# One ring of six PSUM banks for both scans, in-place token loads, and a reordered first stage in a hybrid block kernel

## The chip, the cores and the metric

The program runs on one core of one Trainium2 chip. Its engines are TensorE (PE in the profile, with PEld for its weight loads), VectorE (DVE), ScalarE (ACT), GpSimd (POOL) and SyncE (SP); SP, ACT and POOL also issue transfers between HBM and the on-chip memory. The metric is device time in microseconds (us), lower is better.

## The reference

One layer over 2048 latent tokens and 256 context tokens of width 1024. Cut to what matters:

```python
p_lat = (_layer_norm(h_x) * (1.0 + sc_l[:, None]) + sh_l[:, None]) @ w_in[l]     # sc, sh: silu(c) @ mod_w + mod_b
p_ctx = (_layer_norm(h_ctx) * (1.0 + sc_c) + sh_c) @ w_in[l]
pv, u, fh, g = _split_proj(p)                                   # pooling, RWKV-7, HGRN2, gates
u = _shift3(u, rwkv_shift)                                      # a 3-tap convolution over tokens
y = _rwkv_branch(u_ctx, u_lat, ...)                             # two directions, state from the context
o = _hgrn_branch(fh_ctx, fh_lat, ...)                           # two directions, chunkwise, state from the context
pool = _pool_branch(pv, True, pool_w, pool_scale)
mix = concat([pool, y, o]) * silu(g)
new_x = _layer_norm(ALPHA * h_x + gt * (mix @ w_out)) * ln_g + ln_b

# RWKV-7, one token:  S = S * w - (S kk) (kk * a)^T + v k^T ;  y = S r
# HGRN2, one chunk:   S = exp(g_last) * S + (k * exp(g_last - g))^T i ;  o = (q * exp(g)) S + causal scores i
```

## The kernel before

All matrix products of the projections are made in three passes of a rounded high part and a rest (`wh`, `wl` of the weights; `xh`, `xl` of the tokens), so each 128x1024 block of weights is loaded, cast on ACT and subtracted on DVE or POOL before it is used.

**First stage** (lines 220 to 514). The modulation vector is `silu(c) @ mod_w`: eight loads `mt` of 1 MB on SP's queue into a pool of three buffers, four matmuls each (L241), 16 small transposes (L252), giving `mods`. Then 9 groups of 256 tokens: `x_group` normalizes, transposes on PE (L296) and scales with `mods` into `xm`; `split_group` makes `xh` and `xl`; `conv_block` makes 24 matmuls (L330) for each of 11 blocks of RWKV inputs, `low_rank(d, p, ...)` two small matmuls on the 64 partitions of direction `d` (L347), and further functions the decays, keys and values of each chunk, stored to DRAM (`s_kr`, `s_bk`, `s_vt`). The order here is made by the compiler's scheduler. In the first group each block's weights are loaded just before its `conv_block`, into the pool of three buffers that the token tiles `xt` share.

**RWKV scan** (lines 666 to 974). 36 chunks of 64 tokens in both directions at once. `start` makes the 128x384 score tiles (matmuls L720 into two PSUM banks `pa`, masked by DVE into `at`, L722) seven chunks ahead; `gather` and `solve` invert the triangular blocks of four chunks together in 62 dependent DVE operations (L777, L780) with transfers `sd`, `m`, `so`, `nn` around them; `merge` (L829, L839) and `late` (L742) finish a chunk's factors in banks of the same pool `psa` of two; `step` is the recurrence (`py` L856 and L862, `pu` L872, L881, L897, then `tz` and `zbd` on DVE) in pools `psy` and `psu` of two banks each. PE's order is written out by hand, the other engines are ordered by the scheduler. Between the pieces, `filler` makes the remaining 22 blocks of the input projection (pooling, HGRN2 inputs, gates) in three parts of 768 tokens: it loads tokens `fxs` with two buffers, splits them into `fxh`/`fxl`, and makes 24 matmuls `fps` (L567) for each block and token range. `pace` decides how many of its pieces (six matmuls each) are run per iteration: 7.6 by `R_FIL`. A border between two parts ends the piece.

**HGRN2 scan** (lines 979 to 1181). Ten iterations `n` of 14 slots: `hlevels` for window `n` (`scores`, matmuls L1043 in `pl`; POOL and DVE at L1072), `hsteps` for window `n-1` (L1087, L1102, L1105, L1115 in `pa`, `po`, `ps`, from four pools of 2, 1, 1 and 2 banks). `H_FIL` is the filler's rate per slot; the rest of the filler runs at `n` = 8. `out_weights` loads `w_out`, scales it on POOL and splits it, also at `n` = 8.

**Output stage** (lines 1184 to 1307). `readout` normalizes and gates a group of 512 tokens, `project_out` makes one tile of 128 tokens: matmuls with `w_out`, layer statistics, scaling on ACT (L1290) and POOL (L1291, L1292), one store.

## Time and profile before

| what | us |
|---|---|
| median of 3 runs | 2161.99 (2156.2 to 2167.65) |
| the profiled execution | 2169.2 |
| its span, first to last instruction | 2167.3 |
| first matmul of the first stage's blocks | 53.07 |
| recurrence of the first chunk starts | 652.1 |
| recurrence of the last chunk starts | 1388.6 |
| output stage alone, from about | 1950 |

Times on the engines are counted from the start of the span. A line such as L829 is a line of the kernel before.

### The profile page before, as it was taken

To read this page: it belongs to the slowest core of one execution; us is meant where nothing else is said; L and a number is where in the kernel's file an instruction comes from. 1 tells how busy PE (TensorE), PEld (TensorE's weight loads), DVE (VectorE), ACT (ScalarE), POOL (GpSimd) and SP (SyncE) were. 2 spreads that over 40 slices of the span, in tenths; PEclk is the share of its full clock that TensorE was granted. 3 is DMA by queue.
4 is the path that set the end of the run, shared out by engine and by line. 5 is a ranking of instruction groups with operands and counts; after the bars stand their busy time and mean duration, and the time that the engine had idled before them with its cause. 6 is when DMAs were issued, how large, how long until landed. Compare 5 with 4: busy or idle time off the path is not lost.

```text
span 2167.3 us, 46917 instructions
## 1 busy us (share of the span) xinstructions
PE 1866.9 (86%) x18498; PEld 1581.6 (73%) x18498; DVE 1439.7 (66%) x3037; ACT 930.9 (43%) x1763; POOL 797.8 (37%) x729
## 2 busy tenths in 40 slices
PE   3788899994979988989889897989999998869996
PEld 1677788892857767878768775877787877758886
DVE  2678898885266475675484763167976777669762
ACT  3876786653213333333323233445455555223331
POOL 0144355545211332232232331454443445324653
PEclk7899999996989998999989897999998995589998
DMA  6544444327545567556545544443232333346531
GB/s 245 183 143 146 141 129 126 106 74 237 163 132 149 165 173 202 154 167 177 151 133 167 141 117 139 142 131 90 78 105 80 98 108 109 124 141 199 184 127 59
DMA packets 285156, 305.32 MB, mean 141 GB/s; under 512 B 84932, under 2 KB 243780, under 8 KB 283912
## 3 DMA queue, kind: packets, MB, share of 16 engines
q1 hardware_dynamic: 274920, 271.90, 42.1%
q10 hardware_dynamic: 4896, 17.83, 2.4%
q0 software_dynamic: 5120, 12.59, 1.9%
q8 instruction: 146, 2.39, 0.5%
q14 instruction: 74, 0.61, 0.1%
HBM read 205.49 MB, written 96.74 MB: 139 GB/s over the span
## 4 chain that ended last, share of the span: by engine, by line
PE 33%; DVE 23%; DMA 9%; issue 4%; ACT 3%; POOL 3%; SPq 1%; POOLq 0%; DVEq 0%; ACTq 0%
PE fps L567 14%; DVE o L780 5%; DVE tm L777 4%; PE po L1278 2%; PE pl L1043 2%; DVE sbd L1120 2%; PE po L1105 1%; DMA m<-sd 1%; DVE tot L1075 1%; PE po L1102 1%; DVE at L722 1%; PE py L856 1%; DMA nn<-so 1%; PE pa L720 1%; DVE ml L1222 1%
## 5 line engine op out<-in xcount | busy, mean ns | idle before, releaser
L214 POOL TENSOR_TENSOR fwl<-fwf,fwh 128x1024 fp32r<-128x1024 f32 x66 | 160.1, 2426 | 398.1 <-ACT fwh L213 299.0
L567 PE MATMUL fps<-fxh,fwh 128*128 128x256 f32 (+1 forms) x952 | 228.6, 374 | 29.8 <-ACT fxh L213 22.1
L567 PE MATMUL fps<-fxl,fwh 128*128 128x256 f32 (+1 forms) x952 | 222.1, 365 | 0.0
L567 PE MATMUL fps<-fxh,fwl 128*128 128x256 f32 (+1 forms) x952 | 214.5, 360 | 0.4 <-POOL fwl L214 0.4
L567 PEld LDWEIGHTS fps<-fxh,fwh 128*128 128x128 f32 x952 | 159.1, 200 | 60.5 <-ACT fxh L213 25.5
L567 PEld LDWEIGHTS fps<-fxl,fwh 128*128 128x128 f32 x952 | 160.8, 199 | 27.2 <-issue 4.6
L567 PEld LDWEIGHTS fps<-fxh,fwl 128*128 128x128 f32 x952 | 159.4, 198 | 25.9 <-issue 0.7
L1120 DVE SCALAR_TENSOR_TENSOR sbd<-sbd,tot,ps 64x64 f32<-64x64 f32 x432 | 120.4, 279 | 54.4 <-PE ps L1115 44.1
L1038 ACT COPY qb<-qp 64x384 f32<-64x384 f32 x192 | 99.8, 520 | 120.9 <-PE pl L1043 90.2
L902 POOL TENSOR_TENSOR ys<-ys,pp 64x384 f32<-64x384 f32 x64 | 74.1, 1158 | 199.5 <-ACT ys L899 187.7
L330 PE MATMUL ps<-xh,wh 128*128 128x258 f32 x768 | 125.6, 304 | 18.1 <-ACT wh L213 12.4
L780 DVE TENSOR_TENSOR o<-o,tm 96x31 f32<-96x31 f32 (+15 forms) x279 | 130.6, 468 | 8.1
L777 DVE TENSOR_TENSOR tm<-m,o 96x31 f32<-96x31 f32 (+15 forms) x279 | 109.6, 393 | 36.6 <-DMA m<-sd 29.0
L330 PEld LDWEIGHTS ps<-xh,wh 128*128 128x128 f32 x768 | 106.1, 198 | 31.3 <-ACT wh L213 13.8
L722 DVE TENSOR_TENSOR at<-pa,cst 128x384 f32<-128x384 f32 x144 | 74.1, 548 | 78.3 <-PE pa L720 78.0
L330 PE MATMUL ps<-xh,wl 128*128 128x258 f32 x768 | 118.9, 294 | 0.0
L1072 POOL TENSOR_TENSOR ks<-ks,tot 128x384 f32<-128x384 f32 x90 | 86.3, 964 | 86.5 <-PE pl L1043 78.9
L330 PE MATMUL ps<-xl,wh 128*128 128x258 f32 x768 | 116.2, 290 | 0.0
L1043 PE MATMUL pl<-qb,ks 128*64 128x64 f32 x2304 | 102.4, 248 | 13.4 <-POOL ks L1072 9.9
L821 DVE STREAM_TRANSPOSE nn<-nn 32x192 f32<-32x192 f32 x36 | 13.2, 367 | 146.6 <-DMA nn<-so 138.1
L330 PEld LDWEIGHTS ps<-xh,wl 128*128 128x128 f32 x768 | 104.9, 196 | 5.7 <-issue 5.2
L1043 PEld LDWEIGHTS pl<-qb,ks 128*64 128x64 f32 x2304 | 88.6, 158 | 24.7 <-POOL ks L1072 10.5
(230 smaller groups left out, 4441.9 us busy)
## 6 DMA issues: line engine op xcount, KB each, us to landing
fwf<-in_w_in_dram SPq DMA_DIRECT2D x66, 512.0 KB, 4.1
xt<-in_x_dram ACTq DMA_DIRECT2D x32, 512.0 KB, 5.0
s_kr<-kr SPq DMA_DIRECT2D x54, 256.0 KB, 2.4
s_bk<-bk SPq DMA_DIRECT2D x54, 256.0 KB, 2.5
bks<-s_bk SPq DMA_DIRECT2D x72, 192.0 KB, 2.8
krs<-s_kr SPq DMA_DIRECT2D x72, 192.0 KB, 3.0
bk<-s_bk SPq DMA_DIRECT2D x72, 192.0 KB, 2.7
kr<-s_kr SPq DMA_DIRECT2D x72, 192.0 KB, 3.2
```

What stands on the lines that cost most here:

```text
L214: eng.tensor_tensor(out=wl, in0=wf, in1=wh.bitcast(F32), op=ALU.subtract)
L330: PE.matmul(ps[:, 0:TG + 2], a[:, k, :], b[:, k, :], start=(i == 0), stop=(i == 23))
L567: PE.matmul(ps[:, 0:n], a[:, k, :], b[k][:, o:o + n], start=(i == 0), stop=(i == 23))
L722: V.tensor_tensor(out=at[:, h], in0=pa[h], in1=cst[:, C_MASK[d]].unsqueeze(1).broadcast_to([P, NPR, P]), op=ALU.mult)
L777: V.tensor_tensor(out=tv, in0=m[:, j:j + 1, j + 1:32].broadcast_to([nrow, na, nb]), in1=o[:, 0:na, j:j + 1].broadcast_to([nrow, na, nb]), ...
L780: V.tensor_tensor(out=o[:, 0:na, j + 1:32], in0=o[:, 0:na, j + 1:32], in1=tv, op=ALU.subtract)
L902: G.tensor_tensor(out=ys[vr], in0=ys[vr], in1=pp[d][vr], op=ALU.add)
L1038: S.copy(out=qb[hh, :, :, h, :].rearrange("q p c (i b) -> q (p c) i b", b=b), in_=src[hh].rearrange("q p (c i j b) -> q (p c) i j b", c=nc ...
L1043: PE.matmul(pl[64 * (c % 2):64 * (c % 2) + 64, :, p, c // 2, :], ks[:, p, CH * c:CH * c + CH], qb[:, p, c, :, :], start=True, stop=True)
L1072: eng.tensor_tensor(out=v_, in0=v_, in1=tv[:, :, :, 1 - par:2 - par].broadcast_to([P, NPR, nb, b]), op=ALU.mult)
L1120: V.scalar_tensor_tensor(out=sn[hh, p, hh], in0=so_[hh, p, hh], scalar=tot[hh, p, c:c + 1], in1=ps[hh, p, :], op0=ALU.mult, op1=ALU.add)
L1278: PE.matmul(po, mix[k][a][:, tj], wo[k, 0][b][:, 0:512], start=(i == 0), stop=(i == 23))
```

## The change

Nothing that is computed changes. In the first stage the modulation pool has four buffers instead of three; the transposes of the first token group are placed behind the modulation, and the weights of the first two blocks behind its last load; later blocks' weights are loaded two blocks ahead into a pool of their own (`wf`, two buffers). `low_rank` now makes both directions together, their matmuls in turn. The filler loads six of its eight token slices straight into the tiles `fxl`, where the split leaves the rest later; the two slices that stay in `fxs` are loaded one part ahead. Its rates change. In both scans all PSUM tiles other than the filler's two banks come from one pool of six. `out_weights` works on two column ranges, 256 columns at `n` = 4 and 5 and 768 columns at `n` = 8, with the gate row in a tile of its own; `os` has one buffer instead of two. The last tile is scaled in halves by DVE and stored on two queues.

```diff
-R_FIL = (20, 7.6)
+R_FIL = (20, 10, 7.1)
-H_FIL = (2.2, 1.9, 1.0)
+H_FIL = (2.0, 1.8, 0.85)
...
-            mp = pa.enter_context(tc.tile_pool(name="modw", bufs=3, reuse_waits="tile"))
+            mp = pa.enter_context(tc.tile_pool(name="modw", bufs=4, reuse_waits="tile"))
...
-            wf = t4.tile([P, KB, P], F32, name="xt")
+            wf = t4.tile([P, KB, P], F32, name="wf", bufs=2)
...
+            pls = [psx.tile([P, 2, TG], F32, name="px") for _ in range(2)]
             for j, src in enumerate((xw, xa)):
-                PE.matmul(pl[:, j, :], lup[hs, j, P * p:P * p + P], src[hs], start=True, stop=True)
+                for d in range(2):
+                    hs = slice(64 * d, 64 * d + 64)
+                    PE.matmul(pls[d][:, j, :], lup[hs, j, P * p:P * p + P], src[hs], start=True, stop=True)
+            for d in range(2):
+                decays(d, p, pls[d], st)
...
-        xm = x_group(groups[0])
+        with tc.issue_after(last_mt.ins):
+            for blk in order[:2]:
+                load_weights(blk)
+        with tc.issue_after(last.ins):
+            xm = x_group(groups[0])
...
-                if gi == 0:
-                    load_weights(blk)
+                if gi == 0 and bi + 2 < nb_:
+                    with tc.issue_after(first[0]), tc.issue_after(first[1]):
+                        load_weights(order[bi + 2])
...
+            src = xs + [load(part, k, xl[k].bitcast(F32)) for k in range(2, KB)]
             for k in range(KB):
-                split(xs[k % 2][:, 0:n_all], xh[k][:, 0:n_all], xl[k][:, 0:n_all], V)
-                if k + 2 < KB:
-                    xs[k % 2] = load(part, k + 2)
-                elif pi + 1 < len(parts):
-                    xs[k % 2] = load(parts[pi + 1], k % 2)
+                split(src[k][:, 0:n_all], xh[k][:, 0:n_all], xl[k][:, 0:n_all], V)
+                if k == 1 and pi + 1 < len(parts):
+                    xs = ahead(parts[pi + 1])
...
-        psa = ph.enter_context(tc.tile_pool(name="psa", bufs=2, space=PSUM, reuse_waits="tile"))
-        psy = ph.enter_context(tc.tile_pool(name="psy", bufs=2, space=PSUM, reuse_waits="tile"))
-        psu = ph.enter_context(tc.tile_pool(name="psu", bufs=2, space=PSUM, reuse_waits="tile"))
+        psa = ph.enter_context(tc.tile_pool(name="psa", bufs=6, space=PSUM, reuse_waits="tile"))
+        def bank(shape, **k):
+            return psa.tile([P, 512], F32, name="pa")[:, 0:NPR * P].rearrange(shape, **k)
...
-                py.append(psy.tile([P, NPR, 2, CH], F32, name="py"))
+                py.append(bank("q (p h e) -> q p h e", p=NPR, h=2))
...
-            pace(k * R_FIL[1])
+            pace(k * R_FIL[1 if n < 0 else 2])
...
-        psl = ph.enter_context(tc.tile_pool(name="psl", bufs=2, space=PSUM, reuse_waits="tile"))
-        pst = ph.enter_context(tc.tile_pool(name="psk", bufs=1, space=PSUM, reuse_waits="tile"))
+        pst = ph.enter_context(tc.tile_pool(name="psk", bufs=6, space=PSUM, reuse_waits="tile"))
-        pso = ph.enter_context(tc.tile_pool(name="pso", bufs=1, space=PSUM, reuse_waits="tile"))
-        pss = ph.enter_context(tc.tile_pool(name="pss", bufs=2, space=PSUM, reuse_waits="tile"))
...
-                        os_ = stp.tile([P, 384], F32, name="os")
+                        os_ = stp.tile([P, 384], F32, name="os", bufs=1)
...
+                    if n in (4, 5) and si % 3 == 1:
+                        run(ow1, 1)
...
+            if (g, j) == (gs[-1], 3):
+                for hf, q in enumerate((SP, S)):
+                    c = slice(512 * hf, 512 * hf + 512)
+                    V.scalar_tensor_tensor(out=xt[:, c], in0=xt[:, c], scalar=mu, in1=lng[:, c], op0=ALU.subtract,
+                                           op1=ALU.mult)
+                    V.scalar_tensor_tensor(out=xt[:, c], in0=xt[:, c], scalar=rs, in1=lnb[:, c], op0=ALU.mult,
+                                           op1=ALU.add)
+                    q.dma_start(out=out[P * ti:P * ti + P, c], in_=xt[:, c])
+                return
```

On PE, the program's beginning is before (`pt` are the token transposes, `pm` the modulation, `ps` the first blocks):

```order
L296 MATMUL pt<-cst,xt 128x128 x8
L241 MATMUL pm<-mt,sil 2x512 x32
L252 MATMUL pmt<-cst,mr 128x2 x16
L296 MATMUL pt<-cst,xt 128x128 x10
L330 MATMUL ps<-xh,wh_223 128x258 x8
```

and with the change:

```order
L241 MATMUL pm<-mt,sil 2x512 x32
L252 MATMUL pmt<-cst,mr 128x2 x16
L297 MATMUL pt<-cst,xt 128x128 x18
L332 MATMUL ps<-xh,wh_223 128x258 x8
L332 MATMUL ps<-xh,wl_234 128x258 x8
L332 MATMUL ps<-xh,wh_222 128x258 x8
```

The eight transposes that stood ahead of the modulation stand behind it.

On SP's queue, where the first stage ends and the filler's first part is loaded, there stands before (`fxs` are token slices, `s_kr`, `s_bk`, `s_bon` stores of the first stage, `fwf` a block of filler weights):

```order
L529 DMA fxs<-s_x 128x256
L529 DMA fxs<-s_x 128x512
L707 DMA bks_6265<-s_bk 128x384
L708 DMA krs_6264<-s_kr 128x384
L707 DMA bks_6270<-s_bk 128x384
L708 DMA krs_6269<-s_kr 128x384
L529 DMA fxs<-s_x 128x256
L529 DMA fxs<-s_x 128x512
L733 DMA bk_6929<-s_bk 128x384
L734 DMA kr_6928<-s_kr 128x384
L217 DMA fwf<-in_w_in_dram 128x1024
```

and with the change, ahead of all of these loads but the next `fwf`:

```order
L424 DMA s_bk<-bk 128x4x128
L542 DMA fxl_6035<-s_x 128x512
L542 DMA fxl_6036<-s_x 128x256
L542 DMA fxl_6036<-s_x 128x512
L542 DMA fxl_6037<-s_x 128x256
L542 DMA fxl_6037<-s_x 128x512
L542 DMA fxs<-s_x 128x256
L542 DMA fxs<-s_x 128x512
L542 DMA fxs<-s_x 128x256
L725 DMA bks_6005<-s_bk 128x384
L726 DMA krs_6004<-s_kr 128x384
```

The slices of the first part no longer alternate with the scan's loads; they go out in one run behind the last stores.

On PE in the HGRN2 scan, iteration `n` = 7, there stands before (`pl` are scores, `po` outputs, `ps` state updates):

```order
L1102 MATMUL po<-it_19641,sc_19930 64x64 x6
L1105 MATMUL po<-sbd_16281,qp_19925 64x128 x3
L1115 MATMUL ps<-it_19641,kt_20604 64x64 x6
L1043 MATMUL pl<-qb_16286,ks_20268 64x2x32 x12
L1102 MATMUL po<-it_19641,sc_19930 64x64 x6
L1105 MATMUL po<-sbd_16282,qp_19925 64x128 x3
```

and with the change:

```order
L1120 MATMUL pa<-it_19561,sc_19850 64x64 x6
L1123 MATMUL pa<-sbd_16240,qp_19845 64x128 x3
L1133 MATMUL pa<-it_19561,kt_20534 64x64 x6
L1061 MATMUL pa<-qb_16245,ks_20188 64x2x32 x12
L583 MATMUL fps<-fxh_15217,fwl 128x256
L583 MATMUL fps<-fxh_15218,fwl 128x256
L583 MATMUL fps<-fxh_15219,fwl 128x256
L583 MATMUL fps<-fxh_15220,fwl 128x256
L583 MATMUL fps<-fxl_15221,fwh 128x256
L583 MATMUL fps<-fxl_15222,fwh 128x256
```

Filler matmuls now stand between the scan's pieces in this iteration. Counted on PE's whole list, the filler's matmuls from the first `start` to the first recurrence are 420 instead of 318, between the first and the last chunk's recurrence 1440 instead of 1548, and in the HGRN2 scan 72 in each of `n` = 3 to 6 and 66 at `n` = 7, where it was 84, 84, 84, 72 and none.

## Rows read from the trace of the kernel before

**Rows 1.** The page's first part: busy time, share of the span, instructions.

```profile
span 2167.3 us, 46917 instructions
PE 1866.9 (86%) x18498; PEld 1581.6 (73%) x18498; DVE 1439.7 (66%) x3037; ACT 930.9 (43%) x1763; POOL 797.8 (37%) x729
```

**Rows 2.** Stages: length, PE, PEld, DVE, ACT, POOL busy (instructions), granted clock, DMA, GB/s.

```profile
0.00:53.07 53.07, 19.04 (x98) 6.45 (x99) 12.26 (x40) 16.84 (x23) 0.97 (x8) 0.80 0.67 249
104.79:515.00 410.21, 366.94 (x2610) 325.78 (x2608) 354.86 (x741) 283.22 (x575) 206.00 (x270) 0.96 0.45 132
562.00:652.10 90.10, 74.09 (x517) 61.98 (x517) 46.38 (x108) 16.01 (x28) 18.19 (x9) 0.89 0.55 157
652.10:1388.60 736.50, 645.64 (x7861) 540.61 (x7860) 443.37 (x993) 244.09 (x515) 206.49 (x183) 0.94 0.55 155
```

**Rows 3.** Timeline of the start: start, length, engine, line, [idle before, releaser].

```profile
15.79 1.54 PE L296 MATMUL pt<-cst,xt 128*128 128x128 f32 x6 [4.36 <-ACT xt L288]
17.27 4.96 PE L241 MATMUL pm<-mt,sil 128*2 128x512 f32 x24
19.21 11.65 SPq L239 DMA_DIRECT2D mt<-in_mod_w_dram  x5
37.88 1.04 PE L241 MATMUL pm<-mt,sil 128*2 128x512 f32 x8 [3.29 <-DMA mt<-in_mod_w_dram]
53.07 2.09 PE L330 MATMUL ps<-xh,wh 128*128 128x258 f32 x8 [5.65 <-ACT wh L213]
```

**Rows 4.** Timeline of PE: the low-rank matmuls, alone and side by side.

```profile
341.43 1.13 PE L347 MATMUL px<-t,lup 64*128 64x256 f32 x4
...
77.62 1.14 PE L347 MATMUL px<-t,lup 64*128 64x256 f32 x8
```

**Rows 5.** PE's waits from 515 to 600: total us, times, longest.

```profile
PE fps L567 <- ACT fxh L213: 16.5, 4, 5.7
```

**Rows 6.** PE's waits from 600 to 1395.

```profile
PE pa L829 <- DVE at L722: 31.4, 12, 5.4
PE pa L720 <- DVE at L722: 12.4, 13, 2.4
PE pa L829 <- DVE nn L821: 11.7, 1, 11.7
PE pa L626 <- DVE at L722: 9.4, 3, 4.3
...
PE pa L597 <- DVE at L722: 8.8, 4, 4.2
...
PE pa L742 <- ACT xx L832: 4.3, 2, 2.9
```

**Rows 7.** Four iterations of the RWKV scan, same columns as rows 2.

```profile
929.70:947.70 18.00, 17.02 (x231) 14.36 (x230) 15.06 (x36) 6.40 (x14) 5.54 (x5) 1.00 0.56 171
947.70:972.90 25.20, 19.73 (x236) 16.58 (x235) 19.65 (x52) 6.40 (x14) 3.49 (x5) 0.93 0.51 147
972.90:989.90 17.00, 16.98 (x231) 14.54 (x230) 5.77 (x13) 5.97 (x14) 6.86 (x8) 1.00 0.69 179
...
1303.90:1338.90 35.00, 23.95 (x210) 19.86 (x211) 15.05 (x27) 10.87 (x21) 3.25 (x4) 0.69 0.56 162
```

**Rows 8.** Iterations n = 4, 5 and 7 of the HGRN2 scan, same columns.

```profile
1618.90:1680.20 61.30, 58.47 (x675) 47.97 (x673) 37.36 (x97) 31.68 (x53) 22.65 (x21) 0.83 0.26 83
1680.20:1730.30 50.10, 49.56 (x675) 40.34 (x674) 39.54 (x95) 28.36 (x50) 23.57 (x21) 1.00 0.32 97
...
1779.30:1846.00 66.70, 55.80 (x589) 46.66 (x589) 49.59 (x113) 30.86 (x57) 33.56 (x24) 0.53 0.36 109
```

**Rows 9.** The chain that ended last: start, length, what; 36 filler matmuls.

```profile
572.31 6.44 PE fps L567 x36
```

**Rows 10.** Timeline of ACT and of POOL at the end.

```profile
2152.51 1.24 ACT L1290 ACTIVATE xt<-xt,nm,ln_rs 128x1024 f32<-128x1024 f32 x1 [0.42 <-DVE nm L1289]
...
2156.24 2.34 POOL L1292 TENSOR_TENSOR xt<-xt,lnb 128x1024 f32<-128x1024 f32 x1
```

More of the change, by code (lines that the diff above doesn't have):

```diff
@@ L523, in filler, with load @@
     def filler(parts, blocks):
-        def load(part, k):
-            xs = fp.tile([P, FTOK], F32, name="fxs", bufs=2)
+        def load(part, k, xs):
             o = 0
@@ L867, in step @@
             yield 1
-            pu = psu.tile([P, NPR, 2, CH], F32, name="pu")
+            pu = bank("q (p h e) -> q p h e", p=NPR, h=2)
             for p, h in heads_:
@@ L877, in step @@
             if n + 1 < NCH:
-                zp = psu.tile([P, 2, NPR, CH], F32, name="pu")
+                zp = bank("q (d p e) -> q d p e", d=2, p=NPR)
                 for d in range(2):
@@ L891, in step @@
             if lat:
-                y2 = psu.tile([P, NPR, 2, CH], F32, name="pu")
+                y2 = bank("q (p h e) -> q p h e", p=NPR, h=2)
                 for p, h in heads_:
@@ L1050, in hlevels @@
             if lat:
-                pd = [psl.tile([P, NPR, nm, CH], F32, name="pl") for _ in range(2)]
+                pd = [bank(384, "q (p m t) -> q p m t", p=NPR, m=nm) for _ in range(2)]
                 for h in range(2):
@@ L1098, in hsteps @@
                     if s % 2 == 0:
-                        po = pso.tile([P, NPR, 2, CH], F32, name="po")
+                        po = bank(384, "q (p h e) -> q p h e", p=NPR, h=2)
                     for p in range(NPR):
@@ L1180, in hybrid_block @@
                         run(stp_[d, n - 1])
+            run(ow1)
             run(ow)
```

63 lines of the change are left out of this document (34 added, 29 removed).

## The prediction

> **What bounds the kernel now.** I read the page's first part first. TensorE is busy for 1866.9 of 2167.3 us (86%), the next engine, VectorE, for 66% [rows 1]. So the end is set by TensorE's work, the clock that it is granted, and about 300 us of gaps. Which of these dominates differs by stage, so the second view is the table of stages [rows 2]. In the first 53 us TensorE is busy for 19.0. From 104.79 to 515 both TensorE (366.9) and VectorE (354.9 of 410.2) are nearly full. In the lead of the RWKV scan TensorE lacks 16 us of 90.1, and in the scan proper 91 us of 736.5, at a granted clock of 0.94.
>
> The third view is who ended each wait. Between the first stage and the scan the filler waits 16.5 us for its own split tokens, four times [rows 5]. In the scan, matmuls that open a new tile in the pool `psa` wait for VectorE to free a bank: the rows of `pa` that VectorE's mask L722 or ScalarE's `xx` end are 31.4 + 12.4 + 9.4 + 8.8 + 4.3 = 66.3 us; 11.7 us more are one wait for data, `nn` [rows 6]. The fourth view is single iterations. Of a group of four, two carry the solving chain on VectorE (18.0 and 25.2 us with 15.06 and 19.65 of VectorE). One without it takes 17.0 us, TensorE busy for 16.98 of it. The iteration in which the filler goes from one part to the next takes 35.0 us at clock 0.69 [rows 7]. In the HGRN2 scan the filled iteration `n` = 5 takes 50.1 us with TensorE at 49.56, the same work at `n` = 4 takes 61.3 at clock 0.83, and `n` = 7, without filler, 66.7 at 0.53 [rows 8]. A filler matmul costs 6.44/36 = 0.18 us at full clock [rows 9].
>
> **The change part by part**, against the profiled execution's 2169.2 us. That lies 7.2 above the median of the three runs, so the sum is shifted by 7.2 at the end.
>
> (a) *Start.* TensorE's queue loses the transposes that waited 4.36 us for ScalarE in front of the modulation; the fourth buffer lets the loads of `mod_w` go out without waiting for a buffer, which ended a wait of 3.29; the first weights no longer come on demand, which ended a wait of 5.65 for `wh` [rows 3]. Together 13.3, so −13. If the cast of `wh` still comes last, the first two remain, −8; if SP's issues (five in 11.65 us) also move up, −16. The weights now wait in SP's queue behind the last `mt`; that is covered by the modulation matmuls and transposes.
>
> (b) *Low rank.* Four such matmuls alone take 1.13 us, and eight in which the two halves of the array overlap take 1.14 [rows 4]. 27 pairs (nine groups, three `p`) could save 27 × 1.12 = 30 us if none overlapped yet. But VectorE is 87% busy in this stage [rows 2], and some already overlap: −5, bounds 0 and −30.
>
> (c) *Filler's start.* Eight slices go out in one run instead of through two buffers in alternation with the splits. The wait is 16.5 [rows 5]; what is late next is the first of the splits themselves, and the next `fwf`, which on SP now stands behind the run. −14, bounds −8 (half of it returns as that wait) and −16.5.
>
> (d) *Rates in the RWKV scan.* 102 more filler matmuls in the lead cost 18.4 us, of which 11.7 fall into the wait for `nn`; 108 fewer in the scan proper give 19.4 [rows 6, 9]. Net −12.7 if all in the scan is on the path; −10, bounds −4 and −12.7.
>
> (e) *One ring of six banks.* A tile of `psa` is now reused after two allocations; with the ring, after six. But the ring also serves the recurrence's five tiles per iteration, so in time the distance grows by much less than threefold. The waits of up to 5.4 us should mostly fit. What is late next is VectorE: a solving pair has 34.7 us of it in 43.2 us, with TensorE at about 34 when nothing stalls [rows 7]. A pair would be almost full on both engines, so VectorE must push some masks into the next two iterations, where it has only 5.77. Of 66.3 I take −45. The lower bound is −25 (about the waits outside L829's 31.4, less a third), the upper one all of it.
>
> (f) *Clock.* The scan's clock is 0.94 [rows 2], and the one full iteration ran at 1.00 while the gapped ones ran at 0.93 and 0.69 [rows 7]. So fewer gaps should give clock back: of 645.6 busy us at most 6%, 39, of which I keep 25 as the bound, since a dip is also seen where nothing stalls (`n` = 4 [rows 8]); −9, bounds 0 and −25. A rule speaks against the ring here. The Trainium skill, "TensorE: Matmul & The Clock Gate", section "A second HAM failure mode: psum-queue depth-cycling", says that cycling PSUM tiles through banks in each iteration makes the engine idle in small gaps often enough that its clock oscillates. This trace agrees only in part: the banks rotate today already, two at a time, and a full iteration still shows 1.00. By the trace the term is −9, by that rule a loss, which is a rival below.
>
> (g) *Part borders.* There are two, the one shown at 35.0 us against 17 to 18 [rows 7]. The new part's slices are loaded earlier, but SP issues twelve transfers in a row that wait until the last matmuls release `fxl`, and the splits still queue behind solves on VectorE: −10 for both, bounds −4 and −16.
>
> (h) *HGRN2 scan.* `n` = 7 should come to `n` = 5's 50 us with 66 filler matmuls: its own 589 instructions are what `n` = 5 has without filler, 49.56 − 84 × 0.18 = 34.4 us, plus 11.9, is 46.3, and its VectorE work of 49.6 us then limits it. That is −16.7. 36 fewer filler matmuls at `n` = 3 to 5 give −6.5; the twelve left over at `n` = 8 cost 2; the dip at `n` = 4 (61.3 against 50.1) may or may not go, and that is now where 256 columns of `w_out` are split [rows 8, 9]. Ideal −33; I take −20, bounds −8 and −33.
>
> (i) *Last tile.* ScalarE's 1.24 and two POOL operations of 2.34 each [rows 10] become four half operations on VectorE. At POOL's pace these take 4.7, at best near nothing, and the first half's store starts early: −3, bounds −1 and −5.
>
> (j) *New waits that the trace does not show.* `os` with one buffer makes each copy wait for the store before it, SP's queue has the blocked run of `fxl` loads ahead of chunk loads, and `w_out` comes in sixteen transfers instead of eight. Nothing at best; as much as the longest known data wait, 11.7, and half again at worst, 18; +7, nearer the middle.
>
> Sum: −13 − 5 − 14 − 10 − 45 − 9 − 10 − 20 − 3 + 7 = −122, so 2047 for a profiled execution, and **2040 us** against the median.
>
> **The rivals.**
>
> *The solving chain takes over (0.25).* VectorE's 34.7 us in a pair are a chain of dependent operations with transfers between them, so it cannot be packed, and `nn` then ends the waits that the banks ended. The one wait for `nn` in the lead shows that this happens [rows 6]; against it, it appears only once. Then (e) is −25, (f) 0 and (h) −8: 41 less gain, 2081.
>
> *All at the good ends (0.07).* Bank waits and both clocks come back whole: about −186, 1976. The full iterations at 1.00 speak for it; 10 gains without one cost speak against it.
>
> *The ring ties the recurrence to the masks: slower (0.05).* The tiles `py`, `pu`, `zp` and `y2` had banks of their own. Now the recurrence can wait for a bank that a mask `at`, queued behind solving operations on VectorE, still holds. The price of one such wait is that of today's, 31.4/12 = 2.6 us [rows 6]. With two in each of the 18 solving iterations it is +94, and (e) and (f) come to nothing: +26, or 2188. The other terms are worth 68, so it decides from 68/18 = 3.8 us per solving iteration. Against it, six banks are most of an iteration's tiles, so the mask has some 10 us.
>
> *The clock falls (0.04).* If the ring made the scan run as `n` = 4 does, at 0.83, not 0.94: 0.17 of clock cost 22% there (61.3 against 50.1) [rows 8], so 0.11 cost 14% of some 700 us, about 100. With (f) gone that is −13, or 2149. Beside this stands the rule on cycling banks named at (f).
>
> *It doesn't do what it says (0.03).* The loads wait for buffers where they did, and the ring's slack is taken by the scheduler's order: only (a) and (i) stay, 2146.
>
> **How the numbers follow.** The forecast has 0.56, with a range of its own of 1995 to 2075 (its larger terms, (e), (h), (f), half way to their bounds and partly cancelling). The range 1980 to 2100 takes in the solving-chain rival with some spread; left out are the best case, the slower one, the clock, and the change without effect, together 0.19. Half a per cent, 11 us, is about what a measurement of this kernel tells from no change. Faster: forecast, first two rivals and the part of the last two that lies beyond it, 0.91; same 0.04; slower 0.05.
>
> **What would show it.** (a) The first block matmul near 40 instead of 53.07 us. (c) The wait for `fxh` between the stages below 3 us. (e) The rows of `pa` ended by L722's successor below a third of 66 us in sum, solving pairs near 37 us; if instead `nn` or the recurrence's `pa` grows in the list of waits, the first or third rival holds. (f) The scan's clock at 0.97 or more; below 0.9 is the fourth. (g) The border iterations below 30 us. (h) `n` = 7 near 50 us at clock 0.9 or more. The prediction is wrong if the scan proper, 736.5 us now, takes more than 700 us, or the first stage ends later relative to its start.

## The result and the profile after

The changed kernel takes 2075.4 us (median of four runs, 2061.3 to 2084.9). Its ratio to the kernel before, from runs on the same chip, is 0.9587 (95% interval 0.9522 to 0.9651): 4.1% faster, clearly. The forecast was 2040, 5.6%, so about a quarter of the expected gain did not come. The profiled execution took 2072.9 us, with a span of 2070.8.

The page of the changed kernel, its first part, against [rows 1]:

```profile
span 2070.8 us, 47037 instructions
PE 1835.0 (89%) x18498; PEld 1556.3 (75%) x18498; DVE 1435.9 (69%) x3040; ACT 922.4 (45%) x1759; POOL 796.9 (38%) x735
```

VectorE, ScalarE and POOL do nearly the same work as before, TensorE has the same 18498 matmuls. TensorE's busy time is 32 us less and its idle time 65 us less. No matmul was taken out, so the 32 fit matmuls that ran at a higher clock: the mean over the span is 0.909 before and 0.925 after, 1.8% of 1867 us.

To see where the 96.5 us of span come from I cut both traces at the same instructions: the first block matmul, the last `px` matmul of the first stage, the first `start`, the first and the last matmul with `zbd` (the recurrence), the first matmul of each HGRN2 window (iteration `n`), the last state update. So the scan is counted to the last chunk's own recurrence, 1.3 us further than in the table ahead of the prediction. The last column is the forecast, by its terms.

| stretch | before | after | difference | forecast |
|---|---|---|---|---|
| start, to the first block matmul | 53.1 | 42.9 | −10.2 | (a) −13 |
| first stage | 458.6 | 462.1 | +3.5 | (b) −5 |
| border, to the first `start` | 47.2 | 50.3 | +3.1 | (c) −14 |
| lead | 93.2 | 104.5 | +11.3 | (d) +6.7 |
| RWKV scan | 737.8 | 679.1 | −58.7 | (d) −16.7, (e) −45, (f) −9, (g) −10, together −81 |
| scan to first HGRN2 window | 54.8 | 51.8 | −3.0 | |
| HGRN2, `n` = 1 to 8 | 455.7 | 411.0 | −44.7 | (h) −20 |
| HGRN2, `n` = 9 | 24.4 | 31.7 | +7.3 | |
| output stage | 242.4 | 237.5 | −4.9 | (i), (j) +4 |

The windows of the changed kernel on these cuts, with the columns of [rows 2] and [rows 8] (after the length the busy time of PE, PEld, DVE, ACT and POOL, then clock, DMA share, GB/s): start, first stage, border, lead, scan, then `n` = 4, 7, 8 and 9.

```profile
0.00:42.88 42.88, 20.81 (x99) 5.71 (x99) 10.84 (x36) 17.83 (x25) 1.03 (x8) 0.83 0.84 326
42.88:504.98 462.10, 409.51 (x2834) 363.94 (x2834) 387.36 (x799) 319.27 (x638) 206.87 (x276) 0.93 0.44 132
504.98:555.25 50.27, 31.35 (x123) 23.82 (x121) 7.44 (x19) 11.12 (x14) 13.96 (x9) 0.75 0.61 196
555.25:659.80 104.55, 96.03 (x662) 81.12 (x662) 49.80 (x116) 23.48 (x40) 23.61 (x12) 0.97 0.54 156
659.80:1338.90 679.10, 610.62 (x7753) 515.36 (x7751) 440.95 (x988) 234.93 (x504) 202.02 (x185) 0.95 0.59 166
...
1562.10:1608.63 46.53, 46.53 (x662) 38.40 (x661) 39.74 (x98) 28.99 (x52) 25.01 (x24) 1.00 0.34 103
...
1706.85:1752.08 45.23, 44.85 (x656) 37.06 (x654) 37.51 (x94) 26.38 (x47) 18.48 (x20) 1.00 0.28 86
1752.08:1801.60 49.52, 46.27 (x600) 39.37 (x601) 38.49 (x82) 16.42 (x31) 21.99 (x20) 0.69 0.17 52
1801.60:1833.27 31.67, 28.02 (x256) 21.96 (x252) 15.73 (x47) 6.00 (x11) 9.08 (x8) 0.63 0.39 127
```

And `n` = 8 and 9 before:

```profile
1845.95:1900.45 54.50, 49.90 (x591) 42.37 (x589) 33.69 (x77) 13.07 (x26) 20.69 (x18) 0.61 0.36 124
1900.45:1924.85 24.40, 19.92 (x251) 14.54 (x252) 12.27 (x43) 3.35 (x7) 2.50 (x4) 1.00 0.07 26
```

Three things are to be seen. The start moved 326 GB/s where it moved 249. `n` = 4 and `n` = 7, 61.3 and 66.7 us at clock 0.83 and 0.53 before, are full iterations at 1.00. And the low clock has not gone from the end of this scan: it stands in `n` = 8 and 9 at 0.69 and 0.63. The `n` = 9 says little of the change, though: before it ran at 1.00, but in the three later kernels that keep the old code of this scan it took 31.5 to 32.6 us at 0.55 to 0.58.

The timeline of the start, first and last block of the modulation and the first block matmul, against [rows 3]:

```profile
12.15 1.89 PE L241 MATMUL pm<-mt,sil 128*2 128x512 f32 x8 [12.15 <-DMA mt<-in_mod_w_dram]
...
29.79 1.79 PE L241 MATMUL pm<-mt,sil 128*2 128x512 f32 x8 [0.61 <-DMA mt<-in_mod_w_dram]
...
42.88 2.09 PE L332 MATMUL ps<-xh,wh 128*128 128x258 f32 x8 [1.45 <-ACT xh L308]
```

The modulation begins 5 us earlier, never waits more than 1.44 us for `mt` after its first load, and its last matmuls come at 29.79 instead of 37.88. The weights no longer end the last wait. The first stage behind it gives part of this back. Before, its longest wait but one was 6.6 us for weights `wh`; now one of 8.8 us for the tokens stands at almost the same place:

```profile
PE px L387 <- DVE xh L321: 8.8, 1, 8.8
```

The stage took 459.3 to 465.9 us in the ten kernels of this document with the new order and 456.7 to 458.6 in the four with the old one, so its +3.5 us is more than scatter.

At the border, TensorE's waits from 500 to 662 us (total, times, longest), against [rows 5] and the wait for `nn` in [rows 6]:

```profile
PE fps L583 <- ACT fwh L213: 17.0, 4, 15.1
PE px L437 <- DVE t L433: 6.6, 1, 6.6
PE pa L847 <- DVE nn L839: 6.3, 1, 6.3
```

The 16.5 us of waiting for `fxh` are gone, and 15.1 us of waiting for the first weight block `fwh` stand in their place. SP's queue shows why. Before, the load of that block went out between the token loads:

```profile
501.59 0.46 SPq L217 DMA_DIRECT2D fwf<-in_w_in_dram  x1
...
504.07 0.92 SPq L529 DMA_DIRECT2D fxs<-s_x  x2
```

After, it is the last of a run:

```profile
506.94 2.54 SPq L542 DMA_DIRECT2D fxl<-s_x  x5
509.57 1.32 SPq L542 DMA_DIRECT2D fxs<-s_x  x3
...
513.32 0.32 SPq L542 DMA_DIRECT2D fxs<-s_x  x1
513.72 0.40 SPq L217 DMA_DIRECT2D fwf<-in_w_in_dram  x1
```

It goes out 12 us later, though the stage before ended 6.7 us earlier.

TensorE's waits in the scan, against [rows 6]:

```profile
PE pa L738 <- DVE at L740: 21.8, 6, 5.7
PE pa L642 <- DVE fe L639: 13.6, 2, 7.6
PE pa L890 <- ACT pp L884: 12.7, 9, 5.5
PE pa L847 <- DVE nn L839: 5.4, 1, 5.4
```

The masks still end 21.8 us of waits. They now hold back only the score matmuls L738, no longer the merge or the filler's transposes. But 13.6 us of waits for `fe` stand on the line (L642, L626 before) where 9.4 us ended with a mask: the pooling blocks' own VectorE work. They lie in the 21st and 22nd iteration, 28.0 and 27.1 us long. With the pools apart (below) these two take 26.7 and 28.5, so the ring gains nothing there. And the pair of solving iterations that [rows 7] show at 18.0 and 25.2 us is hardly shorter, with 34.8 us of VectorE in it where it had 34.7:

```profile
915.90:933.50 17.60, 16.77 (x230) 14.24 (x228) 12.51 (x30) 6.39 (x14) 5.37 (x5) 1.00 0.52 149
933.50:958.10 24.60, 19.55 (x229) 16.51 (x229) 22.31 (x48) 5.99 (x13) 5.44 (x5) 0.86 0.53 153
```

### The profile page after: what moved, and what is told of

It reads as the page before. It is cut to its first block, busy times and chain, and to the rows that moved or that the text cites. A ratio compares the mean times of both kernels' runs of the same rounds, so it can differ in the third digit from the quotient of the medians.

```text
span 2070.8 us, 47037 instructions
## 1 busy us (share of the span) xinstructions
PE 1835.0 (89%) x18498; PEld 1556.3 (75%) x18498; DVE 1435.9 (69%) x3040; ACT 922.4 (45%) x1759; POOL 796.9 (38%) x735
## 3 DMA queue, kind: packets, MB, share of 16 engines
q1 hardware_dynamic: 276072, 271.64, 43.7%
## 4 chain that ended last, share of the span: by engine, by line
PE 50%; DVE 19%; DMA 7%; issue 4%; ACT 2%; POOL 2%; SPq 1%; DVEq 0%; ACTq 0%; POOLq 0%
PE fps L583 18%; PE ps L332 3%; PE pa L1061 3%; PE po L1300 2%; DVE tm L795 2%; PE pa L738 2%; DVE o L798 2%; PE pa L874 2%; PE pa L1123 2%; PE pa L1120 2%; PE pa L880 2%; DVE sbd L1138 2%; PE pa L890 2%; PE po L1304 1%; PE po L1302 1%
## 5 line engine op out<-in xcount | busy, mean ns | idle before, releaser
L583 PEld LDWEIGHTS fps<-fxh,fwh 128*128 128x128 f32 x952 | 156.9, 197 | 54.3 <-ACT fwh L213 19.0
L1138 DVE SCALAR_TENSOR_TENSOR sbd<-sbd,tot,pa 64x64 f32<-64x64 f32 x432 | 120.6, 279 | 37.8 <-PE pa L1133 27.7
L795 DVE TENSOR_TENSOR tm<-m,o 96x31 f32<-96x31 f32 (+15 forms) x279 | 114.7, 411 | 39.2 <-DMA m<-sd 31.3
L798 DVE TENSOR_TENSOR o<-o,tm 96x31 f32<-96x31 f32 (+15 forms) x279 | 120.4, 432 | 7.9
L332 PEld LDWEIGHTS ps<-xl,wh 128*128 128x128 f32 x768 | 103.3, 194 | 5.1 <-issue 3.0
L1061 PE MATMUL pa<-qb,ks 128*64 128x64 f32 x2304 | 92.5, 233 | 6.9 <-POOL ks L1090 3.5
L412 POOL TENSOR_TENSOR kr<-t 128x256 f32<-128x256 f32 x54 | 47.1, 871 | 130.0 <-ACT t L399 65.1
```

The source lines that it names most:

```text
L332: PE.matmul(ps[:, 0:TG + 2], a[:, k, :], b[:, k, :], start=(i == 0), stop=(i == 23))
L412: G.tensor_tensor(out=kr[:, :, pr], in0=c4(kk), in1=e_k, op=ALU.mult)
L583: PE.matmul(ps[:, 0:n], a[:, k, :], b[k][:, o:o + n], start=(i == 0), stop=(i == 23))
L795: V.tensor_tensor(out=tv, in0=m[:, j:j + 1, j + 1:32].broadcast_to([nrow, na, nb]), in1=o[:, 0:na, j:j + 1].broadcast_to([nrow, na, nb]), ...
L798: V.tensor_tensor(out=o[:, 0:na, j + 1:32], in0=o[:, 0:na, j + 1:32], in1=tv, op=ALU.subtract)
L1061: PE.matmul(pl[64 * (c % 2):64 * (c % 2) + 64, :, p, c // 2, :], ks[:, p, CH * c:CH * c + CH], qb[:, p, c, :, :], start=True, stop=True)
```

## The experiments

Two kernels can differ by some us in a stretch in which their code is the same: with the same HGRN2 code, `n` = 1 to 8 took 404.8 to 420.7 us in seven runs and `n` = 9 took 27.5 to 36.2; the scan took 672.8 to 679.5 us in six runs that differ in it at most by where weights are loaded. A single stretch is read with that in mind.

**Weights ahead of tokens** (on the changed kernel):

```diff
+        nxt = weights(blocks[0][0])
         xs = ahead(parts[0])
         for pi, part in enumerate(parts):
+            if pi:
+                nxt = weights(blocks[0][0])
             ...
-            nxt = weights(blocks[0][0])
```

> The changed kernel, but the filler's first weight block of each part is loaded ahead of that part's token slices on SP. Theory 1 (order on the queue): the in-place loads did what they should, and the wait for fxh was replaced by a 15.05 us wait for fwh, only because the first fwf stands behind the run of token loads. Then the wait for fwh at the border falls below 4 us, the stretch from the last first-stage matmul to the first start is 36 to 40 us instead of 49.65, and the time is about 10 us under the changed kernel's 2075. Rival (transfers or the last splits limit): the tokens then arrive later by the weight's transfer, fxh or fxl waits come back with 10 us or more, and the stretch stays within 4 us of 49.65.

Ratio 0.9515 (0.9501 to 0.9529), 2064.7 us. The border takes 43.7 us instead of 50.3. TensorE's waits there:

```profile
PE px L437 <- DVE t L433: 6.5, 1, 6.5
...
PE fps L586 <- ACT fwh L213: 5.8, 1, 5.8
PE fps L586 <- ACT fxh L213: 5.0, 3, 2.4
```

The wait for the first `fwh` is gone, so theory 1 has the cause right. It has the size only half right: the 5.8 us are for the second block, which still stands behind the run, and 5.0 us of waiting for `fxh` came back.

**Also the second block** (on the kernel above):

```diff
-            src = xs + [load(part, k, xl[k].bitcast(F32)) for k in range(2, KB)]
+            src = xs + [load(part, k, xl[k].bitcast(F32)) for k in range(2, 5)]
+            after_ = weights(blocks[1][0])
+            src += [load(part, k, xl[k].bitcast(F32)) for k in range(5, KB)]
```

> The changed kernel with the first weight block of each part ahead of its token slices, as in the earlier run, and the second one between the fifth slice and the sixth. Theory 1: the wait of 5.8 us for the second fwh that stayed there goes too, the stretch between the stages falls from 43.7 to 37 to 40 us, the ratio is about 0.949. Rival: the loads of the last slices, now later by that block's transfer, give it back as waits for fxh; the stretch stays at 42 to 45 us, ratio 0.951 to 0.953.

Ratio 0.9546 (0.9518 to 0.9574), 2059.2 us. The border takes 37.3 us, with 0.6 us of waiting for `fwh` left. The first stage is 465.9 instead of 461.4 us in this run, so from the program's start to the first `start` the two differ by 1.6 us (546.0 and 547.6; the changed kernel 555.3). In a further run with the same code up to there (the last but one below) the first stage took 462.0 us and the first `start` came at 540.8, so the longer stage is scatter. Theory 1 holds for the stretch, but not for its ratio of 0.949. The intervals of the two kernels overlap with each other and, at 0.9522 to 0.9529 and up to 0.9574, with the changed kernel's. So the gain at the border is shown in the stretch; in the whole program, where the medians lie 11 and 16 us below the changed kernel's on other chips, it is not.

**Old token loads** (changed kernel, all eight slices through `fxs` again):

```diff
-            src = xs + [load(part, k, xl[k].bitcast(F32)) for k in range(2, KB)]
             for k in range(KB):
-                split(src[k][:, 0:n_all], ...)
+                split(xs[k % 2][:, 0:n_all], ...)
+                if k + 2 < KB:
+                    xs[k % 2] = one(part, k + 2)
```

> The changed kernel with the filler's token loads as before: all eight slices through the two buffers fxs, each loaded when a split frees one. Theory 1 (the loads are worth little where the filler starts, and much at the two part borders): the stretch between the first stage and the first start stays within 4 us of 50.3, the RWKV scan goes from 679.1 to 695 to 705 us, all of it in the two iterations with a border (18.5 and 23.5 us go to 28 or more). Rival (what the scan gained beside ring and rates is the sum of small waits everywhere): the border iterations stay under 26 us and the scan within 8 us of 679.

Ratio 0.9570 (0.9539 to 0.9600), 2070.8 us: no different from the changed kernel. The border is 47.2 us, the scan 679.4 where it was 679.1. Theory 1 fell for the scan. Its local part is seen: the first border's iteration takes 27.3 us, and 18.6 with the in-place loads:

```profile
746.20:773.50 27.30, 17.88 (x236) 14.92 (x234) 18.61 (x37) 12.34 (x23) 7.63 (x6) 0.71 0.77 228
```

But the gain is given back within two iterations: the one two further on takes 20.8 us here and 25.6 in the changed kernel. A reading that fits, but was not tested, is that VectorE works off its queue while TensorE stands at the border.

**The ring and the rates in the RWKV scan, each alone and both.** Pools apart is the changed kernel with 2 + 2 + 2 banks in this scan; old rates is the changed kernel with the rates of before in both scans:

```diff
-        psa = ph.enter_context(tc.tile_pool(name="psa", bufs=6, space=PSUM, reuse_waits="tile"))
+        psa = ph.enter_context(tc.tile_pool(name="psa", bufs=2, space=PSUM, reuse_waits="tile"))
+        psy = ph.enter_context(tc.tile_pool(name="psy", bufs=2, space=PSUM, reuse_waits="tile"))
+        psu = ph.enter_context(tc.tile_pool(name="psu", bufs=2, space=PSUM, reuse_waits="tile"))
```

> The changed kernel with the RWKV scan's PSUM pools as before (2 + 2 + 2 banks), all else as changed. Theory 1 (the ring is worth about a third of the forecast 45): the scan from first to last recurrence, 677.8 us, becomes 695 to 710, and the list of waits gets its rows ended by the masks back at about 60 us against 21.8. Rival A (the ring is worth what was forecast): 720 us or more. Rival B (the gain in the scan came from the moved filler work and the part borders alone): 677 to 685, and the waits on masks stay near 20 us, since they belong to VectorE's queue and not to the banks.

Ratio 0.9623 (0.9589 to 0.9658); the scan takes 692.5 us, 13.4 more, a little under theory 1's 695. The masks end 51.0 us of waits again, 36.5 of them at the merge.

```diff
-R_FIL = (20, 10, 7.1)
+R_FIL = (20, 7.6, 7.6)
-H_FIL = (2.0, 1.8, 0.85)
+H_FIL = (2.2, 1.9, 1.0)
```

> The changed kernel with the filler's rates of before in both scans. Theory 1 (rates carry the HGRN2 gain): the filler runs dry before the last window, which goes back to 60 us or more at a clock near 0.5, and the ten iterations are 430 us or more; in the lead the wait for nn comes back with about 10 us; the whole is 20 to 35 us over 2075. Rival (rings carry it): the whole is within 10 us of 2075.

Ratio 0.9683 (0.9641 to 0.9725), about 21 us over the changed kernel: theory 1. The lead is 93.0 us, the scan 700.5. In the HGRN2 scan, `n` = 7 is back at 65 us and a clock of 0.62, with no filler in it:

```profile
1729.27:1794.32 65.05, 51.53 (x589) 42.16 (x589) 49.29 (x104) 28.64 (x50) 32.36 (x25) 0.62 0.41 134
```

`n` = 1 to 8 take 437.1 us there, but `n` = 9 and the output stage 21.4 and 230.2, against 31.7 and 237.5 in the changed kernel. Of the 26 us that the rates gain in the eight iterations, 17.6 are given back behind them. Counted from the first HGRN2 window to the end of the span, this run takes 688.7 us, and six runs with the changed HGRN2 code and the new last tile take 676.5 to 689.0 (the changed kernel 680.2, the kernel before 722.6). So at the end of the program the HGRN2 rates' gain is not clear of scatter.

From the other side, the kernel before with the ring alone, in the RWKV scan only (the diff above turned round), and with the RWKV rates alone:

> The kernel before with only the RWKV scan's PSUM pools made one ring of six. Theory 1 (the ring alone is worth some 13 us, as its removal cost 13.4): the scan goes from 737.8 to 720 to 728 us, and waits that masks end move from the merge's matmuls to the score matmuls, at 30 us or more still. Rival A (forecast's 45): 700 us or less. Rival B (the ring pays only with the other parts): within 5 us of 737.8. The rest of the program is unchanged, so the total follows: 10 to 18 us, 15 to 45, or nothing.

> The kernel before with only the filler's rates in the lead and in the RWKV scan changed. Theory 1 (the rates move more than the moved matmuls: they shift where filler work, borders and solves meet, and with that take away waits for banks that the ring would otherwise remove): the scan goes from 737.8 to 690 to 705 us, the lead from 93.2 to about 106, and the waits ended by masks in the scan fall from 62 to below 45 us. Rival (the moved work alone, as the difference of 21.4 with the ring in place): 713 to 720 us in the scan, waits for masks as before.

And both together:

> The kernel before with the ring of six and the new rates in the RWKV scan, nothing else. Theory 1 (these two carry all of the scan's gain, token loads nothing): the scan takes 673 to 681 us as in the changed kernel, the program 35 to 55 us less than before. Rival (another part, the token loads or the state in which the scan is entered, carries the 15 us that ring alone, 22.5, and rates, 21.4, leave of 58.7): 690 to 698 us.

Ratios 0.9900 (0.9857 to 0.9942), 0.9861 (0.9830 to 0.9893) and 0.9770 (0.9727 to 0.9813). The scan in the three, columns as above; first the ring alone:

```profile
651.99:1367.28 715.29, 642.77 (x7872) 540.62 (x7871) 441.22 (x993) 242.84 (x515) 206.18 (x183) 0.94 0.56 160
```

the rates alone:

```profile
659.57:1357.97 698.40, 621.82 (x7753) 521.48 (x7751) 443.74 (x988) 235.87 (x504) 201.82 (x185) 0.93 0.57 161
```

and both:

```profile
661.77:1340.31 678.54, 613.98 (x7752) 518.40 (x7751) 439.28 (x988) 235.50 (x504) 198.29 (x181) 0.94 0.58 166
```

From 737.8 the ring takes 22.5 us (between its theory 1 and rival A), the rates 39.4 (theory 1), both 59.3, which is nearly their sum and all of the changed kernel's 58.7. So theory 1 holds for the last of the three: on top of ring and rates, the token loads and the state in which the scan is entered add nothing.

With the rates of before they do. The changed kernel with old rates takes 700.5 us for the scan, the ring alone 715.3, and the largest single difference is the iteration with the second part border, 35.0 us in [rows 7]. First the ring alone, then the changed kernel with old rates:

```profile
1279.94:1316.29 36.35, 23.89 (x210) 19.59 (x211) 13.71 (x27) 10.38 (x20) 3.62 (x4) 0.67 0.53 157
1269.85:1294.14 24.29, 21.29 (x211) 18.01 (x212) 14.05 (x26) 7.99 (x16) 3.43 (x4) 0.78 0.57 159
```

With the rates alone, and the old loads, this iteration takes 26.7 us. So the in-place loads, the only change of the second kernel at a border, and the new rates gain much the same time there, and what a part is worth depends on the others: the ring 22.5 us alone, 19.9 on top of the rates and 13.4 in the changed kernel, the rates 39.4, 36.8 and 21.4.

Of the rates' 39.4, 108 × 0.18 = 19.4 are matmuls that went elsewhere; 11.3 come back in the lead. TensorE's idle time in the scan falls by 14 us, from 90.9 in [rows 2] to 76.6. The masks end fewer waits in the kernel with the rates alone, and ScalarE's `xx` more:

```profile
PE pa L829 <- DVE at L722: 31.7, 12, 4.7
PE pa L742 <- ACT xx L832: 9.1, 2, 8.5
...
PE pa L597 <- DVE at L722: 7.2, 2, 5.4
...
PE pa L720 <- DVE at L722: 2.8, 6, 1.3
```

Over the same stretch as [rows 6], from 600 us, the masks end 47.4 us where they ended 31.4 + 12.4 + 9.4 + 8.8 = 62.0, and `xx` 9.1 where it ended 4.3. So a smaller rate takes 15 us of mask waits away, of which 5 come back as waits for `xx`; theory 1 of that run named the direction and, with below 45, a little more. Why it does was not isolated.

The ring alone leaves other waits:

```profile
PE pa L721 <- DVE at L723: 29.2, 9, 6.7
PE pa L873 <- ACT pp L867: 17.6, 9, 5.9
PE fps L567 <- ACT fxh L213: 10.2, 4, 4.5
```

It takes 33 us of mask waits away, 29 of them in the scan proper, and the scan gains 22.5. In the kernel before, the wait for `pp`, inside the recurrence, was 8.9 us and that for `fxh` 5.6. The 13 us more on these two lines take part of the gain back.

**Half the solve** (changed kernel; every second of the 31 steps is left out, so the result is not the inverse):

```diff
             for j in range(31):
                 na, nb = j + 1, 31 - j
+                if j % 2:
+                    yield 1
+                    yield 1
+                    continue
```

> The changed kernel with every second step of the triangular inversion left out (15 of 31 steps, 30 of 62 VectorE operations in each of the nine groups), so the solved blocks are not the inverse. About 9 x 30 x 0.42 = 114 us of VectorE time are gone. Theory 1 (VectorE's solving operations, ahead of the masks and the state updates in its queue, now bound the scan): the scan falls from 679.1 to 630 to 650 us and the solving iterations of 24 to 28 us come to 20 or less. Rival (the waits are set by the order of tiles in the ring or by the filler, not by VectorE's load): the scan stays above 665 us.

Ratio 0.9454 (0.9434 to 0.9473). The scan takes 656.0 us, the lead 95.1 instead of 104.5. This lies between the two: the solving iterations did come down (the 11th, 15th and 19th from 24.5, 24.7 and 24.8 to 17.0, 17.4 and 17.6, of which the next ones took back 0.3, 2.8 and 4.1), but the 21st and 22nd stayed at 27.8 and 26.9. TensorE's waits in the scan say why:

```profile
PE pa L894 <- ACT pp L888: 13.8, 11, 4.2
PE pa L642 <- DVE fe L639: 13.4, 2, 7.3
PE pa L738 <- DVE at L740: 8.2, 6, 2.3
```

The masks' 21.8 us have become 8.2 and the wait for `nn` is gone from the list; `fe` and `pp` did not move. So VectorE's solving is behind 14 of the 22 us of mask waits and the waits for `nn`, and it sets the length of the solving iterations; `fe` and `pp` do not come from it.

**HGRN2 pools apart** (changed kernel, banks 2 + 1 + 1 + 2 as before in that scan):

```diff
-                pl = bank(384, "q (h p m t) -> q h p m t", h=2, p=NPR, m=nm)
+                pl = psl.tile([P, 2, NPR, nm, CH // 2], F32, name="pl")
...
```

> The changed kernel with the HGRN2 scan's PSUM pools as before (2 + 1 + 1 + 2 banks), all else as changed. Theory 1 (the gain of 45 us in this scan came from filler in the last window and from the full clock that it keeps): the ten iterations stay within 10 us of 411, clock 0.92 or more. Rival (the ring made it): 425 to 445 us, with waits of the score matmuls or of the outputs on ScalarE and VectorE for their banks.

Ratio 0.9568 (0.9552 to 0.9584), the same as the changed kernel. `n` = 1 to 8 take 418.1 us at 0.96, `n` = 9 37.5, the output stage 239.7. Theory 1 is borne out as far as the ring goes; that the ring is worth a few us here is not excluded, since runs with the same code differ by 16 us in the eight iterations.

**Less filler in iterations 3 to 7** (on the kernel with both weight blocks early):

```diff
-H_FIL = (2.0, 1.8, 0.85)
+H_FIL = (2.0, 1.8, 0.75)
...
-                        run(fill if si == 0 else ow, None if si == 0 else 1)
+                        if si < 4:
+                            pace(3)
+                        elif si == 4:
+                            run(fill)
+                        else:
+                            run(ow, 1)
```

> The kernel of the run above, with less filler in the HGRN2 iterations 3 to 7 (rate 0.75 for 0.85) and what is left of it spread over the first four slots of iteration 8, not made at once. Theory 1 (the gain of 20 us in iteration 7 was partly given back, since the low clock only moved to iteration 8, at 0.69, and the last one, at 0.63): iteration 8 keeps 0.85 or more and stays under 55 us with 57 more filler matmuls in it, iterations 3 to 7 lose 9 us, and the program is 5 to 12 us faster than the run above. Rival (VectorE's split of the output weights, now later, sets the end): iteration 8, the last one and the output stage together grow by 15 us or more, and the program is the same or slower.

Ratio 0.9583 (0.9554 to 0.9611), 2067.9 us, against 0.9546 on the same chip: about 8 us slower, the rival; the slowest run of that kernel took 2060.9 us, the fastest of this one 2063.3. `n` = 8 keeps 54.3 us with more filler in it, at clock 0.75, but the output stage takes 252.6 us for 235.8. Its first products wait for what ScalarE has to do first (waits from 1729 us on):

```profile
PE po L1310 <- ACT mh L1253: 41.0, 7, 29.4
```

**Low rank and last tile undone** (changed kernel):

```diff
-            for j, src in enumerate((xw, xa)):
-                for d in range(2):
-                    hs = slice(64 * d, 64 * d + 64)
+            for d in range(2):
+                hs = slice(64 * d, 64 * d + 64)
+                for j, src in enumerate((xw, xa)):
...
-            if (g, j) == (gs[-1], 3):
+            if (g, j) == (gs[-1], 4):
```

> The changed kernel with two parts undone that lie far apart: the low-rank matmuls make one direction after the other, and the last tile is scaled as all others. Each is read from its own stretch. Theory 1: the low-rank order is worth nothing that can be seen (first stage's blocks 462.1 us, stays within 2), since VectorE is full there; the last tile is worth 9 us (from its statistics to the end 6.5 us, goes to about 15.8). Rival: the first stage becomes 5 us or more longer, as forecast for the pairs, and the tail is 3 us longer.

Ratio 0.9615 (0.9592 to 0.9638). The first stage's blocks take 461.0 us, against 462.1: the order of the low-rank matmuls is worth nothing here. From the last tile's statistics to the end of the span it is 2085.0 − 2069.2 = 15.8 us, as before the change (2167.3 − 2151.5), against 6.6 in the changed kernel, whose last operations on VectorE and store on ScalarE's queue are these (against [rows 10]):

```profile
2064.23 0.21 DVE L195 BATCH_NORM_AGGREGATE ln_mv<-ln_st 128x2 f32<-128x12 f32 x1
2064.47 1.42 DVE L1314 SCALAR_TENSOR_TENSOR xt<-xt,ln_mv,lng 128x512 f32<-128x512 f32 x2
...
2065.99 1.42 DVE L1316 SCALAR_TENSOR_TENSOR xt<-xt,ln_rs,lnb 128x512 f32<-128x512 f32 x2
```

```profile
2067.44 0.35 ACTq L1318 DMA_DIRECT2D out_dram<-xt  x1
```

## Why the prediction was right, and where it was not

The direction and the range were right, the likeliest value too good by 35 us. That it was not further off is partly luck: (c) and (d) to (g) came 17 and 27 us short, and the HGRN2 scan gave 17 us more than its term. Step by step:

(a) *Start*, −13: −10.2. The mechanism is as said: no wait for `xt` in front of the modulation or for `wh` behind it is left, and the one of 3.29 us for `mt` is at most 1.44. What remains are the `mt` transfers and 1.45 us for `xh`.

(b) *Low rank*, −5: nothing, the bound of 0; undoing it changed nothing. That VectorE's load, which the forecast named, is the reason was not tested. But the first stage became 3.5 us longer, which the prediction had named as a sign of being wrong ("the first stage ends later relative to its start"). What it missed is the wait for `xh` that now stands where one for `wh` stood; of the start's 10.2 us, 6.7 are left at the end of the stage.

(c) *Filler's start*, −14: +3.1. This step failed, and its own words held the reason: "the next `fwf`, which on SP now stands behind the run". I priced that as at most half of the wait; it was all of it. With one and two weight blocks put ahead, the border falls to 43.7 and 37.3 us, the second 10 less than before the change. So the gain was there to be had, and the queue's order took it.

(d) *Rates*, −10 net: −39.4 in the scan and +11.3 in the lead, −28 net, measured alone on the kernel before; in the changed kernel the scan's part is −21.4. The count of matmuls was right. In the lead only 5.4 of the 11.7 us of the wait for `nn` were filled, and 5.4 us of such a wait stand in the scan instead. What was missed is that bank waits and the second border belong to the rate as well, so part of (e)'s 66 us and of (g) went with the rates.

(e) *Ring*, −45: −22.5 alone, −19.9 on top of the rates, −13.4 in the changed kernel. This is the mis-sized term. The lower bound, −25, was nearer. What the forecast named as late next, the masks in VectorE's queue behind solving operations, is what kept 21.8 us (8.2 with half the solve); that waits for `fe` and `pp` would come in the place of others was not in it. Its sign for the masks came, 21.8 us where a third of 66 is 22, but the solving pair did not come near 37 us: 43.2 became 42.2.

(f) *Clock*, −9 in the scan: 0.94 became 0.95, which on some 610 busy us is about 6, and it was 0.94 with the ring alone and with ring and rates. So no gain is shown for the ring, and the 0.97 that was to show the term did not come. The rule against the ring, in the Trainium skill, "TensorE: Matmul & The Clock Gate", section "A second HAM failure mode: psum-queue depth-cycling", finds no support either: tiles going through six banks in place of two left the clock as it was.

(g) *Borders*, −10: nothing in the sum on top of ring and rates. There the loads made the iteration with the first border 8.7 us shorter, and later ones took it back; with old rates the second border alone is 12 us shorter.

(d) to (g) together were forecast at −74 and gave −47.4.

(h) *HGRN2*, −20: −44.7 in `n` = 1 to 8, +7.3 at `n` = 9. `n` = 7 went from 66.7 to 45.2 us, under the 50 that its VectorE work was to allow, since that work itself fell from 49.6 to 37.5: splits of `w_out` for 12.6 us, which ran there before, no longer do. `n` = 4 went from 61.3 to 46.5. The +7.3 at `n` = 9 is no price of the change that can be told from scatter, since kernels with the old code also took 31.5 to 32.6 us there.

(i) *Last tile*, −3: −9.2. The four half operations take 2.84 us together instead of 5.9 on ScalarE and POOL, and the span ends 3.4 us after them, where it ended 8.7 us after POOL's last one. These 5.3 us were not in the forecast; the last section says where they come from.

(j) *New waits*, +7: the output stage without the last tile's gain is 4.3 us longer. Nothing was tested for it, and six runs with its code took 233 to 244 us.

Of the rivals, the solving chain's 2081 is the nearest number, and its prices for (e) and (f) were near. That its sum comes so near is partly luck, since it had (h) at −8. Its mechanism is only half shown: the solving pair keeps its length, comes down with half the solve, and the solve holds back 14 us of mask waits and the `nn` waits, but `nn` did not take the banks' place (11.7 us before, 6.3 in the lead and 5.4 in the scan after). The slower rival did not come: in the changed kernel no matmul of the recurrence waits for a mask, and in the other kernels with the ring one waits at most 2.3 us. The best case's −186 does not follow from the terms: (e), (f) and (h) at their upper bounds and no new waits make −179, or 1983.

What stays open: why a smaller filler rate removes waits for masks, and what carries most of the gain behind the RWKV scan. From the first HGRN2 window to the end it is 42.3 us, of which the last tile is 9.2; neither the rates nor the ring of that scan, taken out one at a time, brings the rest back, and the earlier columns of `w_out` were not tested.

## What to carry to other kernels

A wait that is removed by putting loads together in a run goes to whatever stands behind that run on the same queue; look for the first operand of the next stage there, and put it ahead. Where a wait for a buffer goes, a wait for data may come in the same iterations, and a change of pacing can remove the same waits as more buffers: price the two by a kernel with each alone and one with both, and by taking each out of the finished kernel, since the answers can differ (22.5 and 13.4 us for the ring here). A gain in one iteration of a pipeline that is fed by a full engine tends to be given back within a few iterations, so a stretch is judged as a whole.

## What the runs showed of the hardware

The end of a program was dearer than its last operation, and dearest where that was POOL's. With one store of 512 KB behind two POOL operations the span ended 8.7 us after the last operation in all five kernels that had it (2158.6 to 2167.3 before, 2076.3 to 2085.0 with the last tile undone); with two stores of 256 KB behind VectorE on two queues it was 3.4 us (2067.4 to 2070.8), 3.4 to 3.9 in all nine that have them. The single store itself landed 2.6 us after its issue at 2158.6. What lasted longer is a `DRAIN` that stands at the end of POOL's instructions, before and after (count, shortest, median and longest in ns, first and last start):

```profile
L1353 POOLq DRAIN  x3: 40/93/10304, 2156.2 to 2167.0; - x3
```

```profile
L1385 POOLq DRAIN  x3: 40/93/10369, 2057.9 to 2070.6; - x3
```

The long one ended 7.9 us after POOL's last operation in every kernel here, at 2166.5 before, and all engines' last semaphore instructions stand behind it. In the changed kernel POOL's last operation ends at 2060.4, the drain at 2068.3, and the last store lands behind that, at 2069.5. VectorE scaled a 128x512 half in 0.71 us, POOL the whole 128x1024 in 2.34.

The granted clock fell late in the HGRN2 scan in every run, by how much differed between runs of the same code. With no filler in `n` = 7 it was 0.53 to 0.73 there (five kernels); with filler it was full, 2.4 GHz, in all nine that had some. In `n` = 8 it was 0.61 before and 0.69 in the changed kernel, between the levels of 1.2 and 2.4 GHz, but 0.64 to 0.88 in seven runs with the same code. In the changed kernel TensorE had gaps in the two low iterations (3.3 us of 49.5 and 3.7 of 31.7).
